# A hybrid attention and mixture-of-experts block on one core: narrow projection first, index scores earlier, subtractions from GpSimd to VectorE, and one transposition a projection later

## The chip, the cores and the metric

One core of a Trainium2 chip runs the whole kernel. The metric is the device time in microseconds of one execution. Engines: TensorE (PE, with its weight loads PEld), VectorE (DVE), ScalarE (ACT), GpSimd (POOL) and SyncE (SP), whose queue issues nearly all transfers.

## The reference, cut to what matters

One layer over 256 tokens of width 1024, all in float32:

```python
proj = x @ w_in                       # columns: A's q, c_kv, q_idx, k_idx, w_idx, B's q, k, v, two gates
# A: index scores pick 64 keys per token, then attention over the picked keys in the latent space
logits = relu(einsum('bthd,bsd->bths', q_idx, k_idx))
iscore = einsum('bth,bths->bts', w_idx * IDX_SCALE, logits)
_, sel = top_k(where(admissible, iscore, -inf), 64)
# ... softmax over the selected keys with a distance penalty, times c_kv, times w_uv -> y_A
# B: attention over all keys of earlier chunks, with a relative-position bias -> y_B
merged = sigmoid(gate_A) * (y_A @ w_branch_a) + sigmoid(gate_B) * (y_B @ w_branch_b)
x = layer_norm(ALPHA * x + merged @ w_out)
# top 4 of 32 experts per token, each a clamped SwiGLU with three 1024 x 1024 matrices
x = layer_norm(ALPHA * x + moe(x))
```

## The kernel before

All engines work through queues in the order in which the program is written out by hand; nothing is reordered at run time. SBUF is cut into 27 slots of 1 MB (`slot`, `free`). A list `pending` holds every large weight matrix in chunks of 1 MB, in order of use: 16 chunks of `w_in` (`in0` to `in15`, two per projection), two each of the branch matrices (`bb`, `ba`), four of `w_out` (`wo`), then the 12 chunks of each of 32 experts, some 403 of the 437.5 MB that are read. `load_next` (line 85) issues the next chunk on SP's queue. `pump(reserve)` issues chunks while more than `reserve` slots are left by the program's own count, and `used()` calls it after each chunk that has been multiplied, with the next number of `RESERVE`. A load whose slot is still being read waits in SP's queue, and what stands behind it too.

The projections and the branches are multiplied in a rounded format with correction: `split` writes a rounded copy `hi` (line 182, by ACT's copy at line 178) and the remainder `lo` (line 183), and each product is three matmuls, hi times hi, lo times hi, hi times lo. `ahead(n)` splits weight chunks up to number n; `AHEAD` says how far ahead of the chunk in use, and the letter in `LO_ENGINE` which engine subtracts (V for DVE, G for GpSimd). A chunk is two instructions of 128x1024 on ACT and two on the subtracting engine. `LO_MERGED` has the same letters for the merged rows before `w_out`.

The order on TensorE before the experts: `qi`, the index queries from `w_qi` (three of the eight steps over the width in plain float32, line 244, five in split form, line 247); `g0`, a narrow product of 200 columns for `k_idx`, `w_idx` and `c_kv` (line 253); `project_T(0)` (B's q); four transposes `ktr` (line 347) of the normalised `k_idx` and `c_kv`, from which DVE makes `kiT` and `ckT` (line 349); `project_T(1)` (B's k); the index scores (line 333), which ACT passes through relu and DVE sums per head (line 364) and searches for the 64 largest (lines 385 and 386); `kat` and `va` (lines 373 and 377); `project_T(2)` to `project_T(4)` with B's and A's scores among them; `project(5)` (B's values); `turn(sB, 1)`, which transposes B's probabilities (24 transposes, line 446); `project_T(6)`; `attend(vb, 1)` (line 462); `project_T(7)`; `turn(sA, 0)`; the two branches, between whose chunks `attend(va, 0)` stands; `w_out`; router; experts. `normalise` (line 423) divides the exponentials by their sums on DVE ahead of each `turn`.

The loads at the start: `xT` in five pieces on SP's queue and `w_qi` in five on ACT's, side by side; then `g0`, four chunks of `w_in`, and the small `ikgb` and `wuk` on SP's.

Of the kernel before, what the change touches and what calls it, by code (L numbers as in the profile page):

```python
# [15 lines left out]
NT = 2  # L16
D = 1024
KD = 8
# [11 lines left out]
SLOT_BASE = 1000.0  # L30
NSLOT = 27
QI_NATIVE = 3
LO_MERGED = "GVGV"
RESERVE = (4, 3, 3, 3, 4, 5, 3, 3, 3, 1, 3, 3, 3, 2, 3, 1, 2, 4, 3, 1, 5, 1, 1, 1, 0)
AHEAD = (3, 4, 3, 3, 3, 3, 3, 3, 3, 3, 3, 3, 3, 3, 3, 3, 3, 3, 3, 3, 3, 3, 2, 1, 0)
LO_ENGINE = "GVVGGGGGGGGGGVGVGVGVGVVV"
KEYS = (128, 256)
KOFF = (0, 128)

# [11 lines left out]
def body(nc, tc, slots, sm, psp, xT_d, x_d, w_g0, w_qi, w_in, ikgb_d, wuk_d,  # L51
# [7 lines left out]
    def slot(name):  # L59
        state["used"] += 1  # L60
        assert state["used"] <= NSLOT, name
        return slots.tile([128, 2048], F32, name=name, tag="slot")

    def free(n=1):
        state["used"] -= n
# [5 lines left out]
    def bank(name):  # L71
        return psp.tile([128, 512], F32, name=name, tag="ps")
# [7 lines left out]
    def load_next(eng=SP):  # L80
        key, src = pending.pop(0)
        t = slot("ld")
        state["ld"] += 1
        for part, from_ in src(t) if callable(src) else ((t, src),):
            eng.dma_start(part, from_)  # L85
        loaded[key] = t
# [44 lines left out]
    xT_s = slot("xT")  # L131
# [2 lines left out]
    wq = [t.rearrange("p (k c) -> p k c", k=4) for t in wq_s]  # L134
    g0_s = slot("g0")
    g0 = g0_s[:, :1600].rearrange("p (k c) -> p k c", k=KD)
    for k0, n in ((0, 1), (1, 1), (2, 2), (4, 2), (6, 2)):
        SP.dma_start(xT[:, k0:k0 + n, :], xT_d[:, k0:k0 + n, :])
        A.dma_start(wq[k0 // 4][:, k0 % 4:k0 % 4 + n, :], w_qi[:, k0:k0 + n, :])
    SP.dma_start(g0, w_g0)  # L140
    for _ in range(4):
        load_next()


    ident = sm.tile([128, 128], F32, name="ident")
# [3 lines left out]
    kvg = ikgb[:, 2:3]  # L149
    uku_s = slot("uku")  # L150
    SP.dma_start(uku_s[:, 0:1024], wuk_d)
    wr = sm.tile([128, KD, NE], F32, name="wr")
    rrow = sm.tile([1, NE], F32, name="rrow")
    lnc = sm.tile([128, 2, KD], F32, name="lnc")
    wuk = uku_s[:, 0:512]
# [18 lines left out]
    def vcopy(o, i):  # L174
        V.tensor_copy(o, i)

    def acopy(o, i):
        A.activation(o, i, AF.Copy)  # L178

    def split(t, hi, lo, rnd=acopy, sub=G):  # L180

        rnd(hi.bitcast(F32R), t)
        sub.tensor_tensor(lo.bitcast(F32R), t, hi, op=ALU.subtract)  # L183
# [6 lines left out]
    def ahead(n):  # L190

        for key in order[len(halves):n]:
            t = take(key)
            hi, lo = slot("hi"), slot("lo")
            sub = {"V": V, "G": G}[LO_ENGINE[len(halves)]]
            for h in range(2):
                cs = slice(h * 1024, (h + 1) * 1024)
                split(t[:, cs], hi[:, cs], lo[:, cs], sub=sub)
            halves.append((hi, lo))
            done(1)  # L200
# [30 lines left out]
    wqh = [slot("wqh0"), slot("wqh1")]  # L231
    wql = [slot("wql0"), slot("wql1")]
    wqHL = [[t.bitcast(F32R).rearrange("p (k c) -> p k c", k=4) for t in ts] for ts in (wqh, wql)]
    qp = [bank("qi") for _ in range(4)]
    for k in range(KD):
        sl = slice(k * 256, (k + 1) * 256)
        split(xT_s[:, sl], xh_s[:, sl], xl_s[:, sl], vcopy, V)
        if k >= QI_NATIVE:
            sl = slice(k % 4 * 512, (k % 4 + 1) * 512)
            split(wq_s[k // 4][:, sl], wqh[k // 4][:, sl], wql[k // 4][:, sl])  # L240
        for j in range(4):
            js = slice(j * 128, (j + 1) * 128)
            if k < QI_NATIVE:
                PE.matmul(qp[j][:, 0:256], wq[k // 4][:, k % 4, js], xT[:, k, :], start=(k == 0), stop=False)
                continue
            for a, b in THREE:
                PE.matmul(qp[j][:, 0:256], wqHL[b][k // 4][:, k % 4, js], xHL[a][:, k, :],
                          start=False, stop=(k == KD - 1 and b == 1))
    free(6)
    g0ps = [bank("g0ps") for _ in range(NT)]  # L250
    for k in range(KD):
        for tb in range(NT):
            PE.matmul(g0ps[tb][:, 0:200], xT[:, k, tb * 128:(tb + 1) * 128], g0[:, k, :],
                      start=(k == 0), stop=(k == KD - 1))
    free(2)
    V.scalar_tensor_tensor(negd, negd, -1.0, negd, op0=ALU.mult, op1=ALU.min)

    def project(g, sink):
# [14 lines left out]
    def project_T(g, sink):  # L273

        ps = [bank("fm") for _ in range(2)]
        for c in range(2):
            i = IN + 2 * g + c
            ahead(i + 1 + AHEAD[i])
            for j in range(4):
                for k in range(4):  # L280
                    for a, b in THREE:
                        PE.matmul(ps[j // 2][:, j % 2 * 256:j % 2 * 256 + 256], part(i, b, k, 4)[:, j * 128:(j + 1) * 128],  # L282
                                  xHL[a][:, 4 * c + k, :], start=(c + k + a + b == 0 and j % 2 == 0),
                                  stop=(c == 1 and k == 3 and b == 1), skip_group_check=True)
                if c == 1 and j % 2:
                    sink(slice(j - 1, j + 1), ps[j // 2].rearrange("p (j t) -> p j t", j=2))
            used()

    def copy_to(dst):
        return lambda js, p: acopy(dst[:, js, :], p)  # L290

    ahead(AHEAD[0])
    for j in range(4):
        vcopy(qiT[:, j, :], qp[j][:, 0:256])


    kT_s = slot("kidxT_ckvT")
# [39 lines left out]
                     ps.rearrange("p (i n) -> p i n", i=per))  # L337


    qb_s = slot("qb")  # L340
    qbT = qb_s[:, 0:1024].rearrange("p (j t) -> p j t", j=4)
    kbT = qb_s[:, 1024:2048].rearrange("p (j t) -> p j t", j=4)
    project_T(0, copy_to(qbT))
    p = bank("ktr")
    for tb in range(NT):
        for i in range(2):
# [8 lines left out]
    def relu_sink(tb, heads, ps):  # L355
        A.activation(rl[tb][:, heads[0]:heads[-1] + 1:2, :], ps, AF.Relu)

    project_T(1, copy_to(kbT))
    for tb in range(NT):
        head_scores(qiT, lambda j: kiT, tb, relu_sink)  # L360
        sl = slice(KOFF[tb], KOFF[tb] + KEYS[tb])
# [4 lines left out]
    free(2)  # L366

    va = uku_s[:, 1024:2048].rearrange("p (b c) -> p b c", b=2)
    for j2 in range(2):
        p = bank("kat")  # L370
        for jj in range(2):
            j = 2 * j2 + jj
            PE.matmul(p[:, jj * 256:(jj + 1) * 256], wuk[:, j * 128:(j + 1) * 128], ckT, start=True, stop=True)
        acopy(kaT[:, 2 * j2:2 * j2 + 2, :], p.rearrange("p (j t) -> p j t", j=2))
    for sb in range(NT):
        p = bank("va")
        PE.matmul(p, ckT[:, sb * 128:(sb + 1) * 128], wuv, start=True, stop=True)
# [17 lines left out]
        SP.dma_start(t, d)  # L395
    SP.dma_start(b1_s, relb_d[:, 1024:3072])
    SP.dma_start(b0_s[:, 0:1024], relb_d[:, 0:1024])
    project_T(2, copy_to(qaT))


# [13 lines left out]
    def exps(s, w):  # L414
        for tb in range(NT):
            for h in range(H):
                A.activation(s[tb][:, h, :], s[tb][:, h, :], AF.Exp, bias=mx[:, w, tb, h:h + 1],
                             accum_out=sums[:, w, tb, h:h + 1])
# [12 lines left out]
    def gate_sink(w, n):  # L431
        return lambda js, p: A.activation(sg[w][:, 4 * n + js.start:4 * n + js.stop, :], p, AF.Sigmoid)
# [57 lines left out]
    project(5, lambda tb, p: acopy(vb[:, tb, :], p))  # L490
    normalise(sB, 1)
    exps(sA, 0)
    turn(sB, 1)
    free(2)
    project_T(6, gate_sink(1, 0))
    attend(vb, 1)
    normalise(sA, 0)
    project_T(7, gate_sink(1, 1))
    free(2)
    turn(sA, 0)  # L500
    free(2)

# [596 lines left out]
```

## Time and profile before

| | |
|---|---|
| median of 3 runs | 1137.94 us (1136.99 to 1138.29) |
| the profiled execution | 1137.62 us, of which the span of its instructions is 1136.0 us |
| TensorE busy | 1061.2 us (93%) |
| DVE, ACT, POOL busy | 293.4, 228.7, 96.6 us |
| read from memory | 435.48 MB, 384 GB/s over the span |
| mean granted clock of TensorE | 0.985 |

Times in the rows are microseconds from the start of the span unless they are marked ns. A busy TensorE is not one at its peak, since matmuls are pipelined and their ends modelled. The granted clock is 1.00 at 2.4 GHz and 0.50 at 1.2 GHz.

### The profile page before, as it was taken

What the parts mean: (1) busy time and instruction counts of PE and PEld (TensorE: products, weight loads), DVE (VectorE), ACT (ScalarE), POOL (GpSimd) and SP (SyncE); (2) the same over time, 40 slices, a digit from 0 to 9 for tenths busy, and PEclk for the clock granted to TensorE, in tenths of its full rate; (3) what the DMA queues carried; (4) which work ended last, traced back from release to release, by engine and by line L of the source; (5) the groups of instructions that cost most, each with busy time, mean ns of one, the idle gap of its engine ahead of it and who ended that gap; (6) DMA issues with size and microseconds to landing.
All of it is one profiled execution on the core that took longest, in us unless ns stands there. A gap on an engine that the chain in (4) does not pass through costs nothing. (4 is left out here: it accounts for less than half of the span.)

```text
span 1136.0 us, 13723 instructions
## 1 busy us (share of the span) xinstructions
PE 1061.2 (93%) x5599; PEld 535.3 (47%) x5599; DVE 293.4 (26%) x711; ACT 228.7 (20%) x425; POOL 96.6 (9%) x54
## 2 busy tenths in 40 slices
PE   8998999999999999999999988996999999989985
PEld 8997998543434343434343434342434343333432
DVE  5398556322111111111111111111021102011123
ACT  3557542211111111201111101111111111011112
POOL 4675232000000000000000000000000000000001
PEclk9999999999999999999999999998999999998998
DMA  9925477999999999999999999999999999999994
GB/s 361 419 108 221 149 267 293 404 399 420 421 421 421 422 420 421 420 422 421 420 422 421 421 421 421 421 421 419 421 421 421 422 421 421 421 407 421 421 419 173
DMA packets 63932, 437.52 MB, mean 385 GB/s; under 512 B 7252, under 2 KB 7892, under 8 KB 11892
## 3 DMA queue, kind: packets, MB, share of 16 engines
q1 hardware_dynamic: 62998, 434.20, 92.9%
q10 hardware_dynamic: 864, 2.36, 0.6%
q8 instruction: 47, 0.77, 0.3%
q14 instruction: 23, 0.19, 0.0%
HBM read 435.48 MB, written 1.05 MB: 384 GB/s over the span
## 5 line engine op out<-in xcount | busy, mean ns | idle before, releaser
L777 PE MATMUL gu<-ld,wa 128*64 128x512 f32 x1024 | 460.1, 602 | 28.9 <-DMA ld<-in_dram 28.9
L775 PE MATMUL gu<-ld,wa 128*64 128x512 f32 x1024 | 458.9, 601 | 7.0 <-PEq L851 3.8
L809 PE MATMUL y<-ld,wc 128*64 128x512 f32 x992 | 239.2, 596 | 16.3 <-DMA ld<-in_dram 16.3
L775 PEld LDWEIGHTS gu<-ld,wa 128*64 128x64 f32 x1024 | 135.8, 138 | 226.5 <-issue 219.7
L796 DVE TENSOR_TENSOR wc<-tr,wb 128x256 f32<-128x256 f32 x64 | 27.0, 421 | 706.6 <-PE tr L792 706.6
L777 PEld LDWEIGHTS gu<-ld,wa 128*64 128x64 f32 x1024 | 135.2, 138 | 112.7 <-DMA ld<-in_dram 60.3
L809 PEld LDWEIGHTS y<-ld,wc 128*64 128x64 f32 x992 | 77.0, 136 | 164.6 <-issue 122.2
L178 ACT ACTIVATE wb<-gu 128x512 f32<-128x512 f32 x64 | 38.2, 597 | 445.1 <-PE gu L775 232.9
L178 ACT ACTIVATE wc<-y 64x512 f32<-64x512 f32 (+1 forms) x66 | 38.2, 578 | 224.2 <-PE y L809 216.7
L183 POOL TENSOR_TENSOR lo<-ld,hi 128x1024 fp32r<-128x1024 f32 x30 | 76.5, 2575 | 62.6 <-ACT hi L178 50.3
L984 POOL PARTITION_BROADCAST ln<-ln x1 | 2.3, 2298 | 929.0 <-DMA ld<-in_dram 929.0
L651 PEld LDWEIGHTS ga<-wa,x 128*128 128x128 f32 x512 | 61.6, 196 | 12.3 <-issue 12.2
L651 PE MATMUL ga<-wa,x 128*128 128x128 f32 x512 | 64.8, 285 | 0.0
L282 PE MATMUL fm<-xh,hi 128*128 128x256 f32 x224 | 64.3, 287 | 0.0
L282 PE MATMUL fm<-xl,hi 128*128 128x256 f32 x224 | 63.4, 283 | 0.0
L282 PE MATMUL fm<-xh,lo 128*128 128x256 f32 x224 | 63.4, 283 | 0.0
L821 PE MATMUL sum<-wc,wb 128*128 128x512 f32 x120 | 54.0, 592 | 0.0
L178 ACT ACTIVATE hi<-ld 128x1024 fp32r<-128x1024 f32 x48 | 47.5, 1048 | 26.8 <-PE fm L282 12.3
L282 PEld LDWEIGHTS fm<-xh,hi 128*128 128x128 f32 x224 | 42.9, 192 | 0.7 <-issue 0.4
L282 PEld LDWEIGHTS fm<-xl,hi 128*128 128x128 f32 x224 | 43.0, 192 | 0.2 <-issue 0.2
L282 PEld LDWEIGHTS fm<-xh,lo 128*128 128x128 f32 x224 | 43.0, 192 | 0.0
L798 ACT ACTIVATE wa<-wc 128x256 f32<-128x256 f32 x64 | 26.6, 416 | 79.4 <-DVE wc L797 78.8
(235 smaller groups left out, 828.6 us busy)
## 6 DMA issues: line engine op xcount, KB each, us to landing
ld<-in_dram SPq DMA_DIRECT2D x404, 1024.0 KB, 19.8
ld<-in_dram SPq DMA_DIRECT2D x8, 512.0 KB, 13.7
wq<-in_dram ACTq DMA_DIRECT2D x3, 512.0 KB, 7.8
biasB<-in_dram SPq DMA_DIRECT2D x1, 1024.0 KB, 12.1
x<-in_dram SPq DMA_DIRECT2D x1, 1024.0 KB, 6.8
g<-in_dram SPq DMA_DIRECT2D x1, 800.0 KB
xT<-in_dram SPq DMA_DIRECT2D x3, 256.0 KB, 7.5
out_dram<-acc SPq DMA_DIRECT2D x3, 256.0 KB, 2.0
```

The source lines that it names most:

```text
L178: A.activation(o, i, AF.Copy)
L183: sub.tensor_tensor(lo.bitcast(F32R), t, hi, op=ALU.subtract)
L282: PE.matmul(ps[j // 2][:, j % 2 * 256:j % 2 * 256 + 256], part(i, b, k, 4)[:, j * 128:(j + 1) * 128], xHL[a][:, 4 * c + k, :], start=(c + ...
L651: PE.matmul(ps[j // per][:, (j % per) * n:(j % per + 1) * n], x1_cols(tb, j), Pt, start=(tb == 0 and j % per == 0), stop=(tb == 1), skip_g ...
L775: PE.matmul(ps[n][0:64, :], xe(j), wg(j, cs), start=(j == 0), stop=(j == KD - 1), skip_group_check=True)
L777: PE.matmul(ps[n][64:128, :], xe(j), wu(j, cs), start=(j == 0), stop=(j == KD - 1), skip_group_check=True)
L796: V.tensor_tensor(gg, pv[:, :, 0, :], bg(js), op=ALU.add)
L798: A.activation(sg_, gg, AF.Sigmoid, scale=1.702)
L809: PE.matmul(p[64 * n:64 * n + 64, :], hT[:, j, :], wd(j, slice(n * 512, (n + 1) * 512)), start=(j == 0), stop=(j == KD - 1), skip_group_ch ...
L821: PE.matmul(sums[tb][n], lhsT, rhs, start=start, stop=stop, skip_group_check=True)
L984: G.partition_broadcast(ln2_s, ln2_s[0:1, :])
```

## The change

It loads `xT` and `g0` first (`g0` on ACT's queue, `w_qi` behind `xT` on SP's, the four chunks after `wuk`) and multiplies `g0` ahead of `qi`. `ktr`, the split of `in0` and `kat` come before `project_T(0)`; the index scores, the search and `va` come between `project_T(0)` and `project_T(1)`. DVE subtracts 21 of the 24 chunks in place of 9, all of `qi`'s five steps and all four merged groups. `turn(sB, 1)` comes after `project_T(6)` in place of `project(5)`, and `attend(vb, 1)` after `project_T(7)`. Two of the reserves change.

```diff
-LO_MERGED = "GVGV"
-RESERVE = (4, 3, 3, 3, 4, 5, 3, 3, 3, 1, 3, 3, 3, 2, 3, 1, 2, 4, 3, 1, 5, 1, 1, 1, 0)
+LO_MERGED = "VVVV"
+RESERVE = (4, 1, 3, 3, 4, 5, 3, 3, 3, 1, 3, 3, 3, 3, 3, 1, 2, 4, 3, 1, 5, 1, 1, 1, 0)
-LO_ENGINE = "GVVGGGGGGGGGGVGVGVGVGVVV"
+LO_ENGINE = "VVVVVGGGVVVVVVVVVVVVVVVV"
...
-    for k0, n in ((0, 1), (1, 1), (2, 2), (4, 2), (6, 2)):
+    for k0, n in ((0, 1), (1, 1), (2, 2), (4, 4)):
         SP.dma_start(xT[:, k0:k0 + n, :], xT_d[:, k0:k0 + n, :])
-        A.dma_start(wq[k0 // 4][:, k0 % 4:k0 % 4 + n, :], w_qi[:, k0:k0 + n, :])
-    SP.dma_start(g0, w_g0)
-    for _ in range(4):
-        load_next()
+    for k0, n in ((0, 2), (2, 6)):
+        A.dma_start(g0[:, k0:k0 + n, :], w_g0[:, k0:k0 + n, :])
+    for k0, n in ((0, 2), (2, 2), (4, 4)):
+        SP.dma_start(wq[k0 // 4][:, k0 % 4:k0 % 4 + n, :], w_qi[:, k0:k0 + n, :])
...
     SP.dma_start(uku_s[:, 0:1024], wuk_d)
+    for _ in range(4):
+        load_next()
...
+    g0ps = [bank("g0ps") for _ in range(NT)]
+    for k in range(KD):
+        for tb in range(NT):
+            PE.matmul(g0ps[tb][:, 0:200], xT[:, k, tb * 128:(tb + 1) * 128], g0[:, k, :],
+                      start=(k == 0), stop=(k == KD - 1))
+        sl = slice(k * 256, (k + 1) * 256)
+        split(xT_s[:, sl], xh_s[:, sl], xl_s[:, sl], vcopy, V)
+    free(1)
     qp = [bank("qi") for _ in range(4)]
     for k in range(KD):
-        sl = slice(k * 256, (k + 1) * 256)
-        split(xT_s[:, sl], xh_s[:, sl], xl_s[:, sl], vcopy, V)
+        sl = slice(k % 4 * 512, (k % 4 + 1) * 512)
         if k >= QI_NATIVE:
-            sl = slice(k % 4 * 512, (k % 4 + 1) * 512)
-            split(wq_s[k // 4][:, sl], wqh[k // 4][:, sl], wql[k // 4][:, sl])
+            split(wq_s[k // 4][:, sl], wqh[k // 4][:, sl], wql[k // 4][:, sl], sub=V)
...
-    free(6)
-    g0ps = [bank("g0ps") for _ in range(NT)]
-    for k in range(KD):
-        for tb in range(NT):
-            PE.matmul(g0ps[tb][:, 0:200], xT[:, k, tb * 128:(tb + 1) * 128], g0[:, k, :],
-                      start=(k == 0), stop=(k == KD - 1))
-    free(2)
+    free(7)
...
-    ahead(AHEAD[0])
-    for j in range(4):
-        vcopy(qiT[:, j, :], qp[j][:, 0:256])
...
-    project_T(0, copy_to(qbT))
     p = bank("ktr")
...
-    project_T(1, copy_to(kbT))
+    ahead(1)
+    for j in range(4):
+        (acopy if j % 2 else vcopy)(qiT[:, j, :], qp[j][:, 0:256])
+    for j2 in range(2):
+        p = bank("kat")
+        for jj in range(2):
+            j = 2 * j2 + jj
+            PE.matmul(p[:, jj * 256:(jj + 1) * 256], wuk[:, j * 128:(j + 1) * 128], ckT, start=True, stop=True)
+        acopy(kaT[:, 2 * j2:2 * j2 + 2, :], p.rearrange("p (j t) -> p j t", j=2))
+    project_T(0, copy_to(qbT))
     for tb in range(NT):
         head_scores(qiT, lambda j: kiT, tb, relu_sink)
...
+    project_T(1, copy_to(kbT))
     project_T(2, copy_to(qaT))
...
     project(5, lambda tb, p: acopy(vb[:, tb, :], p))
     normalise(sB, 1)
     exps(sA, 0)
+    project_T(6, gate_sink(1, 0))
     turn(sB, 1)
     free(2)
-    project_T(6, gate_sink(1, 0))
-    attend(vb, 1)
     normalise(sA, 0)
     project_T(7, gate_sink(1, 1))
     free(2)
+    attend(vb, 1)
     turn(sA, 0)
     free(2)
```

## Rows read from the trace of the kernel before

**Rows 1.** Busy time by stretch: engines, granted clock, DMA share, rate.

```profile
0.00:60.00 60.00, 56.29 (x405) 52.65 (x406) 27.64 (x60) 28.95 (x42) 33.07 (x24) 0.97 0.96 384
60.00:195.00 135.00, 129.29 (x1032) 121.70 (x1031) 96.31 (x155) 63.22 (x123) 58.34 (x28) 0.97 0.54 204
195.00:1118.00 923.00, 868.47 (x4134) 358.25 (x4132) 160.17 (x484) 133.32 (x255) 1.82 (x1) 0.99 1.01 418
```

**Rows 2.** Waits of TensorE from 420 us on: total, times, longest.

```profile
PE gu L777 <- DMA ld<-in_dram: 28.9, 28, 1.4
```

**Rows 3.** Timeline of TensorE around `turn(sB)` and `project_T(6)`: start, length.

```profile
109.00 0.39 PE L267 MATMUL tm<-lo,xh 128*128 128x512 f32 x1
111.56 0.79 PE L446 MATMUL ptr<-ident,biasB 128*128 128x128 f32 x4 [2.17 <-DVE biasB L423]
...
119.39 0.36 PE L282 MATMUL fm<-xh,hi 128*128 128x256 f32 x1
...
131.07 2.84 PE L462 MATMUL pv<-pt,sa_vb 128*64 128x128 f32 x48
```

**Rows 4.** The same timeline at `turn(sA)` and the first branch.

```profile
145.46 0.60 PE L446 MATMUL ptr<-ident,sa_vb 128*128 128x128 f32 x4
...
148.00 0.48 PE L528 MATMUL br<-y,hi 128*128 128x256 f32 x2
```

**Rows 5.** Busy time by stretch, at the start and at `turn(sB)`.

```profile
16.00:20.00 4.00, 4.00 (x23) 4.00 (x22) 0.00 (x0) 3.07 (x5) 3.20 (x3) 0.57 1.01 419
109.40:119.40 10.00, 4.30 (x25) 3.97 (x25) 8.15 (x5) 8.28 (x35) 4.09 (x2) 0.66 0.00 0
```

**Rows 6.** Timeline of DVE at the two calls of `normalise`.

```profile
108.15 7.48 DVE L423 TENSOR_TENSOR biasB<-biasB,sums 128x1024 f32<-128x1024 f32 x2
...
135.58 1.22 DVE L423 TENSOR_TENSOR sa_vb<-sa_vb,sums 128x1024 f32<-128x1024 f32 x1
136.73 2.28 DVE L423 TENSOR_TENSOR sa<-sa,sums 128x2048 f32<-128x2048 f32 x1
```

**Rows 7.** Timeline of ACT at the last exponential of `sA`.

```profile
116.44 0.49 ACT L417 ACTIVATE sa<-sa,mx 128x256 f32<-128x256 f32 x1
```

**Rows 8.** The subtractions of line 183: ns min/median/max, first and last start.

```profile
L183 POOL TENSOR_TENSOR lo<-ld,hi x30: 2352/2407/5135, 20.1 to 157.9; 128x1024 fp32r<-128x1024 f32 x30
L183 DVE TENSOR_TENSOR lo<-ld,hi x18: 1211/1219/3379, 21.0 to 180.2; 128x1024 fp32r<-128x1024 f32 x18
L183 DVE TENSOR_TENSOR y<-pv,y x4: 691/692/692, 133.4 to 157.6; 128x512 fp32r<-128x512 f32 x4
```

**Rows 9.** Timeline of DVE at the first residual.

```profile
186.64 0.69 DVE L669 SCALAR_TENSOR_TENSOR x<-x,wo 128x512 f32<-128x512 f32 x1 [5.20 <-PE wo L665]
```

**Rows 10.** Busy time by stretch in the first 20 us, rate last.

```profile
0.00:10.00 10.00, 8.06 (x50) 7.24 (x51) 3.10 (x12) 1.91 (x2) 1.69 (x9) 1.00 0.78 252
10.00:20.00 10.00, 8.23 (x46) 7.17 (x45) 5.51 (x11) 4.22 (x7) 6.23 (x5) 0.83 1.02 423
```

**Rows 11.** Timelines of DVE and ACT where they wait for `xT` and `w_qi`.

```profile
9.01 0.29 DVE L175 CAST xh<-xT 128x256 fp32r<-128x256 f32 x1 [1.94 <-DMA xT<-in_dram]
...
16.93 1.15 ACT L178 ACTIVATE wqh<-wq 128x512 fp32r<-128x512 f32 x2 [2.64 <-DMA wq<-in_dram]
```

**Rows 12.** Timelines of TensorE and DVE from `qi` to `ckT`.

```profile
8.59 2.54 PE L244 MATMUL qi<-xT,wq 128*128 128x256 f32 x11
...
22.43 5.58 PE L253 MATMUL g0ps<-g,xT 128*128 128x200 f32 x32
27.70 0.42 PE L282 MATMUL fm<-xh,hi 128*128 128x256 f32 x1
...
39.36 0.60 PE L347 MATMUL ktr<-ident,kidxT_ckvT 128*128 128x128 f32 x4
39.71 0.36 PE L282 MATMUL fm<-xh,hi 128*128 128x256 f32 x1
...
40.46 0.48 DVE L349 TENSOR_SCALAR kidxT_ckvT<-ktr,ikgb 128x256 f32<-128x256 f32 x1
```

More of the change, by code (lines that the diff above doesn't have):

```diff
@@ L337, in head_scores @@
                      ps.rearrange("p (i n) -> p i n", i=per))
-    qb_s = slot("qb")
-    qbT = qb_s[:, 0:1024].rearrange("p (j t) -> p j t", j=4)
-    kbT = qb_s[:, 1024:2048].rearrange("p (j t) -> p j t", j=4)
-    project_T(0, copy_to(qbT))
     p = bank("ktr")
@@ L356, in relu_sink @@
         A.activation(rl[tb][:, heads[0]:heads[-1] + 1:2, :], ps, AF.Relu)
-    project_T(1, copy_to(kbT))
+    ahead(1)
[7 more added lines that the diff above has]
+        acopy(kaT[:, 2 * j2:2 * j2 + 2, :], p.rearrange("p (j t) -> p j t", j=2))
+    qb_s = slot("qb")
+    qbT = qb_s[:, 0:1024].rearrange("p (j t) -> p j t", j=4)
+    kbT = qb_s[:, 1024:2048].rearrange("p (j t) -> p j t", j=4)
+    project_T(0, copy_to(qbT))
     for tb in range(NT):
@@ L368, in body @@
     va = uku_s[:, 1024:2048].rearrange("p (b c) -> p b c", b=2)
[L369 to L374, printed above, removed]
     for sb in range(NT):
```

## The prediction, made before the changed kernel ran

> **What bounds the kernel now.** I read the stretches first: from 195 to 1118 us the DMA engines are busy without a pause, 418 GB/s at share 1.01 [rows 1]. What TensorE waits for after 420 us is those transfers: on the gate and up line alone 28 waits, 28.9 us, none over 1.4 [rows 2]. So the expert weights set the end: it is the moment from which the stream never pauses again, plus bytes that the change leaves alone. Before that moment the stream does pause: from 60 to 195 us its share is 0.54 [rows 1], some 62 us without transfers, because the 27 slots are full and come free only as TensorE finishes chunks. So a microsecond taken out of TensorE's queue before about 200 us should bring the whole stream, and the end, forward by one; work moved between other engines counts only if TensorE waits for it.
>
> Then I read where TensorE loses time before 200 us. One place stands out. The last matmul of `project(5)` ends at 109.39, `turn(sB)` gets its first four transposes off at 111.56, and `project_T(6)` starts at 119.39 [rows 3]: 10.00 us. The same 24 transposes of `turn(sA)` take from 145.46 to 148.00, 2.54 us [rows 4]. The loss is 7.46 us, part of it at half the matrix rate, since the granted clock of the stretch is 0.66 and TensorE's busy time 4.30 of 10; the DMA share there is 0.00 [rows 5], so the stream stands still with TensorE. What is late is `normalise(sB)` on DVE: 7.48 us from 108.15 to 115.63, against 1.22 + 2.28 = 3.50 us for the same shapes of `sA` [rows 6]; GpSimd, busy for 4.09 us of the stretch [rows 5], was subtracting beside it.
>
> **The turning one projection later.** `project_T(6)` takes 119.39 to 131.07, 11.68 us [rows 3]. Put ahead of `turn(sB)`, it moves the transposes from 109.39 to 121.07, while `normalise(sB)` ended at 115.63: covered by 5.4 us even at the slow length. I count the whole 7.46 us. What can be late next: ACT ends the exponentials of `sA` at about 117 [rows 7], then rounds `in15` and `bb0` (four instructions, 3.9 us), loads the sigmoid table (1.3) and evacuates `project_T(6)` (2 x 0.6), done at 123.4; `project_T(7)`, which may take those two banks again, starts at 121.07 + 2.54 = 123.6. That holds by 0.2 us, so between nothing and 1 us can come back here; I take nothing, because the first bank is free 0.5 us sooner. `attend(vb, 1)` now ends right before `turn(sA)`; its two casts and two subtractions are four DVE instructions of 0.69 us [rows 8], the first branch chunk reads only the first half, and 2.54 us of transposes lie between. Nothing, or 0.5 us. The pages that hold B's probabilities come free later, which shifts two loads by one projection each, in a stretch where the stream is idle about half the time.
>
> **The subtractions.** 12 of the 24 chunks go from GpSimd to DVE, 24 instructions of 1.22 us = 29.3; seven of half the size (five of `qi`'s, two of the merged rows) at 0.69, 4.8. Together 34 us. GpSimd keeps three chunks, 6 x 2.41 us [rows 8]. DVE is busy 27.6 + 96.3 = 124 us of the first 195 [rows 1]; with 34 added and the 4.0 us excess of `normalise(sB)` taken off, some 154 of 188. It is in-order, so the average doesn't settle it; three places do.
> First, the stretch up to the turning: `in11`, `in12` and `in14` add 3 x 2.44 = 7.3 us in front of `normalise(sB)`. If not one of them fell into idle time, it would end at 115.63 + 7.3 - 4.0 = 118.9, before 121.07. If this cover went, each microsecond would be one of TensorE's.
> Second, the top-k. It starts one projection earlier (11.6 us) and has three more chunks (`in8` to `in10`, 7.3 us) behind it before B's scores need DVE: free 4 us sooner than now.
> Third, the output projection: two merged groups more wait in DVE's queue for ACT's rounding (0.7 each) and subtract (0.7): 2.8 us, so the last chunk's subtraction, which ends at 181.4 now, ends at about 184.2. It is needed some 1.4 us ahead of 186.64, where the residual follows the last matmuls [rows 9]: covered by 1 us. Between nothing and 1 us; I take nothing.
> What speaks against the move is that GpSimd's three remaining chunks run beside the top-k. The longest DVE subtraction took 3.38 us against 1.21 [rows 8]. The Trainium skill (SBUF — State Buffer, Who interferes with whom) says that a DVE instruction with two SBUF inputs and a GpSimd instruction that reads SBUF exclude each other, the later one blocked for the whole of the other; the row agrees. By that rule six GpSimd instructions could hold DVE for 6 x 2.41 = 14.5 us here, an estimate; but the rows that I sum from already hold more GpSimd work beside the same top-k, so the sum is the same either way.
>
> **The start.** Bytes: 2.52 MB had moved by 10 us and the rate is then 423 GB/s [rows 10], so x us moves 0.42 (x - 4) MB. The third piece of `xT` ends 0.52 MB on SP's queue, and its companion of `wq` 1.05 MB on ACT's; it landed at 9.01 [rows 11], 1.3 us after 1.57 MB had moved. In the new order `g0` (0.82 MB, ACT's queue) shares with `xT` (1.05 MB, SP's): at equal shares `g0` is through at 1.64 MB, 7.9 us, and lands at 9.1; `xT` at 9.7. (The last of `wq`, 2.1 MB on ACT's queue, landed at 16.93 [rows 11], when 4.9 MB had moved: a share of 43%, by which `g0` lands at 9.8.) TensorE can do two of eight steps early and starts the other six at 9.1. `g0`'s 16 matmuls took 22.43 to 27.70 [rows 12], 0.33 each, so 12 take 4.0 us: 13.1. `qi`'s 12 native matmuls: 11 records in 2.54 us, so 24 records 5.5 us: 18.6. The 60 rounded ones at the pace of `project_T(6)`, 11.68/96 = 0.122 [rows 3], 7.3 us: 25.9. `wq` is through by 3.97 MB, landed at 14.7, and the rounding and subtraction of its last four steps by 18, so they hide. Then `ktr`, which now has nothing between it and `kat`: transposes at 39.36, `ckT` ready at 40.94, 1.58 us, where before only 0.35 us of TensorE's queue was spent [rows 12]. `in0`'s subtraction now comes behind `ckT` on DVE, 1.2 us to its first half, and `kat`'s four matmuls cover it. Against the first chunk's start now (27.70, plus the 0.35): 28.05 - (25.9 + 1.58) = 0.6 us gained at the full clock.
> But TensorE then idles from about 7 to 9.1 us. Two rows tell what follows a pause of that size: after the idle 13 to 15 us the clock from 16 to 20 us was 0.57 [rows 5], a loss of 0.43 x 4 = 1.7 us, and after 109.39 it fell too. I take the half clock: 0.6 - 1.7 = -1.1 us. Ends: +0.6 with the clock held, -2.6 if `g0` lands 1.5 us later.
> Moving scores and `kat` costs TensorE nothing in itself: the same instructions, with banks evacuated by an ACT that has room there (29 busy of the first 60 us [rows 1]).
>
> **Sum.** 7.46 - 1.1 = 6.4 us, rounded up. From the profiled execution's 1137.62 us (span 1136.0 and 1.6 around it): 1131.2. That execution stands 0.3 us under the median of the runs, 1137.94, so I leave the figure there.
>
> **The rivals.**
> 1. The clock holds at the start (or falls where TensorE waits anyway): 7.46 + 0.6 gives 1129.6.
> 2. The turning still waits: ACT is late with the sigmoids, or DVE's longer queue uses up the 2 us that [rows 6] leave it. A wait of 1 to 4 us gives 1132.2 to 1135.2. For it: DVE has little room in that stretch. Against it: 11.68 us of cover.
> 3. The time is not carried to the end: slots come free as before, by another engine than TensorE, and the stream starts no earlier: 1137.6. Against it: it moved nothing at all in the stall [rows 5].
> 4. Slower, by one mechanism: `g0` on ACT's queue doesn't get half of the rate but is served behind SP's. Behind `xT` and `wq` it would land at 4 + 3.97/0.42 + 1.25 = 14.7 us, 5.6 late, and the gain shrinks to 0.8 us (1136.8); from a landing at 15.5 the kernel is slower; behind `wuk` and `in0` as well (5.54 MB) it lands at 18.4, 9.3 late: 1140.5. Against it: ACT's 43% above [rows 11].
>
> **How the numbers follow.** My forecast, the turning's 7.46 us less 1.1 at the start, 45 in 100; rival 1, 22; rival 2, 20; rival 3 and rival 4 up to its point, 6; rival 4 beyond it, or DVE so late that it outweighs 6.4 us, 7. The range takes the forecast, rival 1 with 0.7 us to spare, and rival 2 up to a wait of 3 us: 1128.8 to 1134.3, 83 in 100 or a little less. A difference of 0.2% (2.3 us) is about what a measurement of this kernel can tell from no change. Faster by more than that: 87; within it: 6; slower: 7.
>
> **What would show it.** Right: `project_T(6)` follows `project(5)` without a gap, `turn(sB)` takes about 2.5 us, `turn(sA)` ends near 141.5 in place of 148.0, and the stream is at share 1.0 from some 6 us sooner; a granted clock under 1 once near 10 us; DVE busy for some 154 us before 190. Wrong: a wait of `ptr` for `sB`, of the first chunk for `lo`, or of `g0ps` for `g0` past 10 us; an equal time with an earlier `turn(sA)` would mean that the stream isn't led by TensorE.

## The result, and the profile after

The changed kernel takes 1127.96 us (median of 4 runs, 1127.57 to 1129.88), the kernel before beside it 1138.08 (4 runs, 1136.99 to 1138.29): a ratio of 0.9916, 95% interval 0.9899 to 0.9934. It is faster, as forecast, but by 10.1 us in place of 6.4; the time lies 0.8 us under the low end of the range. The profiled execution happens to be the longest of the four, 1129.88 us, with a span of 1128.3; a second profile of the same kernel (`after_again`, 1128.07 us) stands beside it below, because the two differ at one place. Helper lines sit two lines further down than before: the subtractions are L185, the transposes L448, `project_T` L284.

The stretches of the changed kernel, columns as in [rows 1]:

```profile
0.00:60.00 60.00, 56.50 (x407) 53.37 (x408) 40.42 (x100) 29.80 (x44) 12.67 (x13) 1.00 0.95 384
60.00:187.00 127.00, 127.00 (x1031) 120.08 (x1029) 100.60 (x143) 62.65 (x123) 7.97 (x8) 1.00 0.58 216
187.00:1110.00 923.00, 870.02 (x4136) 358.17 (x4133) 160.55 (x485) 133.51 (x255) 2.30 (x1) 0.99 1.01 418
```

From 60 to 187 us TensorE has no idle time at all (127.00 of 127; 129.29 of 135 before). The stream of transfers is at share 1.01 over the same 923 us set 8 us sooner than in [rows 1], and has the rate that it had, 418 GB/s. The waits of TensorE, of the first 215 us (the two longest behind the start-up) and, last, from 420 us on:

```profile
PE kat L359 <- issue: 1.1, 1, 1.1
PE g0ps L239 <- DMA xT<-in_dram: 0.6, 1, 0.6
...
PE gu L779 <- DMA ld<-in_dram: 28.7, 26, 1.6
```

No wait of `ptr` is left, and the waits for expert weights are those of [rows 2], 28.7 us against 28.9: the second part of the kernel didn't change, it begins sooner. That can be checked to a few tenths. TensorE's first expert matmul starts at 209.86 in the trace of before, and that execution's whole time is 927.8 us more; in the changed kernel it starts at 202.01, with 927.9 us more to the whole time; in its second profile at 199.97, with 928.1 more:

```profile
199.97 0.64 PE L777 MATMUL gu<-ld,wa 128*64 128x512 f32 x1
```

So the 9.9 us between 209.86 and 199.97 are the gain from trace to trace, and it arises at two places only: before B's turning (the scores of `sA` start at 95.40 before, at 93.18 in the second profile, 2.2 sooner) and at it (from those scores to `turn(sA)`: 50.06 us before, 42.34 in both profiles after, 7.7 less). From `turn(sA)` to the first expert matmul it takes 64.4 or 64.5 us in all fourteen profiles. The 2.2 us are a difference to one trace, though: `turn_only` below, whose start is that of before, has those scores at 93.40.

The turning, timeline of TensorE and, last, of DVE, for [rows 3] and [rows 6]:

```profile
108.83 0.39 PE L269 MATMUL tm<-lo,xh 128*128 128x512 f32 x1
109.05 0.28 PE L284 MATMUL fm<-xh,hi 128*128 128x256 f32 x1
```

```profile
110.19 3.43 DVE L425 TENSOR_TENSOR biasB<-biasB,sums 128x1024 f32<-128x1024 f32 x2
```

The first matmul of `project_T(6)` follows the last of `project(5)` on its heels, where 10.00 us stood. `turn(sB)` starts 11.5 us later, at 120.57, and its 24 transposes take 2.54 us. `normalise(sB)` takes 3.43 us where it took 7.48 and is done at 113.6: 7 us ahead of its reader.

The start is where the two profiles of the changed kernel differ. TensorE in the first, and then in the second (each of `g0`'s 16 matmuls is two records):

```profile
5.04 1.65 PE L239 MATMUL g0ps<-g,xT 128*128 128x200 f32 x4
7.25 6.89 PE L239 MATMUL g0ps<-g,xT 128*128 128x200 f32 x28 [0.56 <-DMA xT<-in_dram]
13.98 1.24 PE L252 MATMUL qi<-xT,wq 128*128 128x256 f32 x5
```

```profile
5.04 1.31 PE L239 MATMUL g0ps<-g,xT 128*128 128x200 f32 x4
6.95 5.15 PE L239 MATMUL g0ps<-g,xT 128*128 128x200 f32 x28 [0.60 <-DMA xT<-in_dram]
11.94 3.40 PE L252 MATMUL qi<-xT,wq 128*128 128x256 f32 x15
```

The wait is the same, 0.6 us, and it is for `xT`, not for `g0`. The 28 records behind it take 6.89 us in one and 5.15 in the other; one microsecond of each, the first profile's and then the second's, shows why:

```profile
10.00:11.00 1.00, 1.00 (x4) 1.00 (x4) 0.93 (x4) 0.00 (x0) 0.00 (x0) 1.00 1.10 459
```

```profile
10.00:11.00 1.00, 1.00 (x8) 1.00 (x7) 0.95 (x3) 0.00 (x0) 0.00 (x0) 1.00 1.12 467
```

Four records a microsecond against eight, TensorE busy all the time: half the rate, until 10.9 us. It isn't the pause that brings it. In the first profile the four records ahead of the pause are as far apart (0.33 us) as those behind it, so TensorE had not come to the full rate yet. Two more profiles of the new start, `after_third` and then `start_only`, have the same four records at the half rate and at the full one, a pause of 0.29 us and one of 1.06, and the full rate behind both:

```profile
5.04 1.65 PE L239 MATMUL g0ps<-g,xT 128*128 128x200 f32 x4
6.98 5.09 PE L239 MATMUL g0ps<-g,xT 128*128 128x200 f32 x28 [0.29 <-DMA xT<-in_dram]
```

```profile
4.94 0.94 PE L239 MATMUL g0ps<-g,xT 128*128 128x200 f32 x4
6.95 5.00 PE L239 MATMUL g0ps<-g,xT 128*128 128x200 f32 x28 [1.06 <-DMA xT<-in_dram]
```

All that follows is 2.04 us later in the first profile, to the end of the kernel. Of eight profiles of kernels that load `g0` in the new way one shows this; of the thirteen executions of the changed kernel itself one, this one, is over 1128.6 us.

The subtractions: DVE is busy 147.4 us of the first 195 in the second profile (154 reckoned, 124 before), GpSimd 20.8 (91.4 before, [rows 1]). The chunks' subtractions in the first profile (busy, mean ns | idle before):

```profile
L185 DVE TENSOR_TENSOR lo<-ld,hi 128x1024 fp32r<-128x1024 f32 x42 | 50.7, 1266 | 7.4 <-ACT hi L180 7.4
```

42 of them at 1.27 us, and none delays TensorE. The last two stand in front of the residual of [rows 9] (timeline of DVE):

```profile
173.39 4.33 DVE L185 TENSOR_TENSOR lo<-ld,hi 128x1024 fp32r<-128x1024 f32 x2 [0.26 <-ACT hi L180]
178.79 0.69 DVE L671 SCALAR_TENSOR_TENSOR x<-x,wo 128x512 f32<-128x512 f32 x1 [1.07 <-PE wo L667]
```

The second of them ends at 177.72, and the matmul that reads it starts at 178.37: 0.65 us to spare, 1 reckoned.

### The profile page after: what moved, and what is told of

Its sections match the earlier page's. It is cut to its first block, busy times and chain, and to the rows that moved or that the text cites. A ratio compares the mean times of both kernels' runs of the same rounds, so it can differ in the third digit from the quotient of the medians.

```text
span 1128.3 us, 13701 instructions
## 1 busy us (share of the span) xinstructions
PE 1060.8 (94%) x5599; PEld 534.3 (47%) x5599; DVE 310.8 (28%) x740; ACT 229.2 (20%) x427; POOL 25.8 (2%) x23
## 5 line engine op out<-in xcount | busy, mean ns | idle before, releaser
L779 PE MATMUL gu<-ld,wa 128*64 128x512 f32 x1024 | 459.3, 601 | 30.8 <-DMA ld<-in_dram 28.7
L284 PE MATMUL fm<-xh,hi 128*128 128x256 f32 x224 | 64.1, 286 | 0.0
L284 PE MATMUL fm<-xl,hi 128*128 128x256 f32 x224 | 63.4, 283 | 0.0
L284 PE MATMUL fm<-xh,lo 128*128 128x256 f32 x224 | 63.4, 283 | 0.0
L185 DVE TENSOR_TENSOR lo<-ld,hi 128x1024 fp32r<-128x1024 f32 x42 | 50.7, 1266 | 7.4 <-ACT hi L180 7.4
L284 PEld LDWEIGHTS fm<-xh,hi 128*128 128x128 f32 x224 | 43.0, 192 | 0.6 <-ACT hi L180 0.3
L284 PEld LDWEIGHTS fm<-xl,hi 128*128 128x128 f32 x224 | 43.0, 192 | 0.3 <-issue 0.2
L284 PEld LDWEIGHTS fm<-xh,lo 128*128 128x128 f32 x224 | 43.0, 192 | 0.0
L794 PEld LDWEIGHTS tr<-ident,wb 128*128 128x128 f32 x256 | 33.3, 208 | 13.7 <-issue 12.6
## 6 DMA issues: line engine op xcount, KB each, us to landing
biasB<-in_dram SPq DMA_DIRECT2D x1, 1024.0 KB, 11.5
```

The source lines that it names most:

```text
L779: PE.matmul(ps[n][64:128, :], xe(j), wu(j, cs), start=(j == 0), stop=(j == KD - 1), skip_group_check=True)
L794: PE.transpose(p[:, i * 128:(i + 1) * 128], gu[:, (j // 2) * 256 + j % 2:(j // 2) * 256 + 256:2], ident)
```

## The experiments

None of these kernels leaves out a part of the computation; `before_warm` only adds matmuls whose result nobody reads. Times are medians; the ratio is to the kernel before, run on the same chip (1138.46, 1138.58 and 1138.22 us in the three groups of runs).

**The changed kernel again.**

> The changed kernel once more, unchanged, for more executions and a second trace. Its profiled execution reached the first expert 7.85 us sooner than before and ended 7.74 sooner, but the median of its runs is 10.1 us lower than that of before. Theory 1 (only TensorE's queue before the experts counts): the trace shows the first expert again 7.8 +- 0.3 us sooner, at about 202.0, and the medians differ by 7.5 to 8.5 with more runs, the rest being scatter of single runs. Theory 2 (the start differs from run to run in what the clock does, and the profiled run was a bad one): the first expert starts 1 to 2 us before 202.0 and the medians differ by 9 to 10.5. Theory 3 (something in the experts' stage gets shorter too): the first expert at 202.0, but the end 2 us sooner than 1128.3 of span, and the medians differ by about 10.

1128.32 us (1127.71 to 1128.5), 0.9911 (0.9897 to 0.9924). The time repeats. Its profile is the one quoted above; the scores of `sA` start at 93.18.

**The turning alone, in the kernel before**, with the one reserve that belongs to it.

```
     exps(sA, 0)
+    project_T(6, gate_sink(1, 0))
     turn(sB, 1)
     free(2)
-    project_T(6, gate_sink(1, 0))
-    attend(vb, 1)
     normalise(sA, 0)
...
     free(2)
+    attend(vb, 1)
     turn(sA, 0)
```

> The kernel before with one part of the change alone: the turning of B after the projection behind it, attend one projection later, the one reserve that belongs to it. Theory 1: 7.46 us at the first expert (202.4), 1130.5 +- 1 of time, so nearly the whole difference; the two normalisations keep their lengths. Theory 2 and 3 with the gain elsewhere: still 7.5 here, and the missing 2 us then come with another part. If the cover failed: a wait of the transposes for normalise and less than 6 us.

1129.95 us (1128.88 to 1131.1), 0.9929 (0.9915 to 0.9943): 8.5 us by the medians. This edit carries most of the whole. From the scores of `sA` to `turn(sA)` it takes 42.34 us, as in the whole change. `normalise(sB)` is as slow as it was, because GpSimd still subtracts beside it (timeline of DVE):

```profile
106.15 7.57 DVE L423 TENSOR_TENSOR biasB<-biasB,sums 128x1024 f32<-128x1024 f32 x2
```

It ends at 113.7, and `turn(sB)` starts at 118.74 without a wait: 5.0 us of cover, 5.4 reckoned.

The start of this kernel is that of before, instruction for instruction, and yet its trace is 2.0 us ahead of that of before when `g0` begins (22.43 in [rows 12]) and when the scores of `sA` do (93.40 against 95.40). The last piece of `w_qi` is there at 15.51 (16.93 in [rows 11]), and the clock holds where [rows 5] has 0.57:

```profile
20.42 5.58 PE L253 MATMUL g0ps<-g,xT 128*128 128x200 f32 x32
```

```profile
16.00:20.00 4.00, 3.48 (x29) 3.28 (x29) 0.50 (x2) 2.97 (x5) 3.78 (x3) 1.00 1.02 422
```

So the old start differs by 2 us from one execution to another, and the trace that the forecast was reckoned from has a late one.

**The subtractions alone, in the kernel before.**

```
-LO_MERGED = "GVGV"
+LO_MERGED = "VVVV"
-LO_ENGINE = "GVVGGGGGGGGGGVGVGVGVGVVV"
+LO_ENGINE = "VVVVVGGGVVVVVVVVVVVVVVVV"
...
-            split(wq_s[k // 4][:, sl], wqh[k // 4][:, sl], wql[k // 4][:, sl])
+            split(wq_s[k // 4][:, sl], wqh[k // 4][:, sl], wql[k // 4][:, sl], sub=V)
```

> The kernel before with the subtractions of the change alone (21 chunks, the five steps of qi and the merged rows on DVE), all orders as before. normalise(sB) should fall from 7.48 to about 3.5 us with GpSimd silent, and end at about 113.6 in place of 115.6. Theory 1: TensorE's stall at the turning shrinks by 2 to 3.5 us, the start by up to 1 us (the wait for wql on GpSimd, 1.0 us, goes), so 1134 to 1136. If DVE's queue is the dearer place (it is longer by 29 us): equal or slower, 1138 to 1140.

1137.35 us (1136.13 to 1138.21), 0.9991 (0.9982 to 1.0). TensorE's timeline at the turning before (the wait for the later transposes, behind the one in [rows 3]), then here, and then DVE's here:

```profile
115.89 3.75 PE L446 MATMUL ptr<-ident,biasB 128*128 128x128 f32 x20 [3.54 <-DVE biasB L423]
```

```profile
112.32 1.09 PE L446 MATMUL ptr<-ident,biasB 128*128 128x128 f32 x4 [4.33 <-DVE biasB L423]
114.51 4.50 PE L446 MATMUL ptr<-ident,biasB 128*128 128x128 f32 x20 [1.11 <-DVE biasB L423]
```

```profile
106.02 4.62 DVE L183 TENSOR_TENSOR lo<-ld,hi 128x1024 fp32r<-128x1024 f32 x4
110.56 0.24 DVE L421 RECIPROCAL sums<-sums 128x16 f32<-128x16 f32 x1
110.83 3.43 DVE L423 TENSOR_TENSOR biasB<-biasB,sums 128x1024 f32<-128x1024 f32 x2
```

`normalise(sB)` is 4.1 us shorter but starts 2.7 later (110.83 against 108.15 of [rows 6]), behind two chunks that GpSimd did before. It ends 1.4 us sooner, but `project(5)` does too. The two waits are 4.33 and 1.11 us in place of 2.17 and 3.54, 5.4 in all against 5.7, and from the scores of `sA` to `turn(sA)` it takes 50.90 us against 50.06: quick DVE work doesn't help while TensorE asks for it right behind `project(5)`.

**The whole change without the new start** (loads as before, `g0` behind `qi`).

```
-    for k0, n in ((0, 1), (1, 1), (2, 2), (4, 4)):
+    for k0, n in ((0, 1), (1, 1), (2, 2), (4, 2), (6, 2)):
         SP.dma_start(xT[:, k0:k0 + n, :], xT_d[:, k0:k0 + n, :])
-    for k0, n in ((0, 2), (2, 6)):
-        A.dma_start(g0[:, k0:k0 + n, :], w_g0[:, k0:k0 + n, :])
...
+        A.dma_start(wq[k0 // 4][:, k0 % 4:k0 % 4 + n, :], w_qi[:, k0:k0 + n, :])
+    SP.dma_start(g0, w_g0)
...
```

> The changed kernel with the start of before: w_qi on ACT's queue beside xT, g0 and four chunks behind, and g0 multiplied after qi; all else as changed. Theory 1: the start before lost 1.7 us to the half clock and 1.7 to waits, and the changed one starts its first projection only 0.25 us sooner, so 0.2 to 1 us slower than the changed kernel, 1128.5 to 1131 beside 1128 to 1130. Theory 2 (the start is worth 2 us more than the profiled run showed): 2 to 3 us slower than the changed kernel.

1136.98 us (1136.16 to 1138.11), 0.999 (0.9981 to 0.9999): 8.7 us above the changed kernel, far outside what either theory said. The timeline of TensorE:

```profile
20.27 5.58 PE L253 MATMUL g0ps<-g,xT 128*128 128x200 f32 x32
29.66 1.22 PE L339 MATMUL ktr<-ident,kidxT_ckvT 128*128 128x128 f32 x4 [3.81 <-DVE kidxT_ckvT L314]
31.95 3.75 PE L357 MATMUL kat<-kidxT_ckvT,uku 128*128 128x256 f32 x8 [1.07 <-issue]
```

With `ktr` next in the queue behind `g0`, TensorE stands 3.81 us for the norms of `g0`'s result and 1.07 for `ckT` (the view names no releaser, but `ckT` is written by 31.85 and `kat` starts at 31.95), and it works at half rate between the two and behind (`kat`'s eight matmuls 3.75 us against 1.97 in the changed kernel). The scores of `sA` start at 101.56, 8.4 us behind `after_again`. The kernel before hid the norms under `project_T(0)`; the changed one hides them under `qi`, which now comes after `g0`. Start and new place of `ktr` and `kat` are one edit, not two.

**The whole change with B's turning in its old place** (the diff of `turn_only` reversed).

> The changed kernel with the turning of B back in its old place (and attend and the one reserve). In the run with only the subtractions moved the stall there was 10.8 us for 2.5 us of transposes, because the longer queue of DVE ends normalise(sB) 6 us behind project(5) although normalise itself is down to 3.4. Theory (the turning is the main gain, and the subtractions need it): the stall returns whole, 6 to 8.3 us slower than the changed kernel, 1134.5 to 1136.8. Rival (the quiet GpSimd had shortened the stall by half on its own): 3 to 4 us slower, 1131.5 to 1132.5.

1134.62 us (1133.63 to 1135.91), 0.997 (0.9961 to 0.9979): 6.3 us above `after_again`. TensorE's waits of the first 215 us:

```profile
PE ptr L448 <- DVE biasB L425: 4.0, 2, 2.5
```

From the scores of `sA` to `turn(sA)` 49.67 us against 42.34, so 7.3 come back, 4.0 of them as this wait and the rest at half rate beside and behind it (granted clock 0.66 from 110 to 120).

**The new start alone, in the kernel before.** The edit is the start's part of the change (printed above): loads, `g0` ahead of `qi`; `ktr`, `kat` and the scores stay.

> The kernel before with the new start alone: xT and g0 loaded and multiplied first, w_qi and four chunks behind; ktr, kat, scores, turning and subtracting engines as before. Theory: no pause of 2 us in the middle of qi, so the loss to waits (1.7) goes always and the one to the half clock (1.7, which fell in the profiled run of before and not in three later ones) goes too: 1 to 2.5 us faster than before in the median, and a narrower spread. Rival (the start is worth what the two first traces differ by): 0.2 us, not to be told from before.

1136.8 us (1135.68 to 1138.49), 0.9985 (0.9976 to 0.9994): 1.7 us, between 0.7 and 2.7. TensorE has the scores of `sA` at 92.78: 2.6 us ahead of the trace of before and 0.6 ahead of `turn_only`, the old start at its better. It is also 0.4 ahead of `after_again`. Of that, 0.15 is an earlier `qi` (11.79 against 11.94); the other 0.25 is what the new places of `ktr`, `kat` and the index scores cost TensorE.

**The kernel before with its TensorE kept busy at the start**, by 24 small matmuls ahead of each of two steps of `qi`.

```
+        if k in (4, 5):
+            warm(24)
         for j in range(4):
```

> The kernel before with 24 more small matmuls on zeros ahead of the fifth and of the sixth step of qi, where TensorE waits for w_qi, and nothing else; the result is not touched by them. It tells the clock from the waits. If the spread of before is the half clock that falls in some runs after that pause: the clock holds at 1.00 in the first 30 us, the slowest runs (1139 to 1140) go, and the median falls by 0.5 to 1.7 us. If the clock has no part in it: same as before or up to 1 us slower.

1138.33 us (1136.96 to 1139.22), 1.0001 (0.9992 to 1.001). The stretch of [rows 5] has its clock, and `g0` comes no sooner all the same (22.43 in [rows 12]):

```profile
16.00:20.00 4.00, 4.00 (x48) 3.96 (x47) 0.00 (x0) 2.94 (x4) 3.06 (x3) 1.00 1.00 412
```

```profile
22.34 5.58 PE L255 MATMUL g0ps<-g,xT 128*128 128x200 f32 x32
```

This run doesn't settle what the clock was worth: the second filler runs from 16.63 to 17.95, while the remainder that the next step reads was ready at 16.83, so it took 1.1 us itself. A better reading is `dve_only`, where the last piece of `w_qi` landed at the same time (16.87 us; 16.93 in [rows 11]) and the clock held by itself: `g0` at 21.02, 1.4 us sooner. There the subtractions of `w_qi` were quicker too, so 1.4 is a bound from above. In `turn_only` GpSimd subtracts as before, the last piece came 1.4 us sooner and `g0` 2.0: that leaves 0.6 for the clock, from one execution of each.

**`kat` later:** in the changed kernel, `ktr` after the first chunk's rounding and `kat` behind `project_T(0)` and the index scores, run twice.

```
+    ahead(1)
     p = bank("ktr")
...
-    ahead(1)
     for j in range(4):
         (acopy if j % 2 else vcopy)(qiT[:, j, :], qp[j][:, 0:256])
-    for j2 in range(2):
...
     va = uku_s[:, 1024:2048].rearrange("p (b c) -> p b c", b=2)
+    for j2 in range(2):
```

> The changed kernel with one thing more: in0 is split ahead of ktr (DVE idles there for 4.5 us), and kat comes behind project_T(0) and the index scores, so that TensorE doesn't wait the 1.07 us between ktr and kat that both traces of the changed kernel show. If only TensorE's queue counts: 1.0 us faster than the changed kernel, about 1127.2, the first project_T starts right behind ktr. Rival: the first chunk's remainder is late instead and the wait only moves: same.

> The kernel with in0 split ahead of ktr and kat behind the index scores once more, beside the changed kernel on one chip: 1.0 to 1.3 us faster than that, as the first experts (198.7 against 200.0) say. If that was the chip or the single run: same.

1127.0 (1126.47 to 1128.06) and 1127.01 us (1126.71 to 1127.58), 0.991 (0.9895 to 0.9925) and 0.9904 (0.989 to 0.9919). TensorE goes from `ktr` into the projection without a pause, and its first expert matmul comes at 198.72 and 198.47:

```profile
24.36 0.60 PE L342 MATMUL ktr<-ident,kidxT_ckvT 128*128 128x128 f32 x4
24.72 0.36 PE L284 MATMUL fm<-xh,hi 128*128 128x256 f32 x1
```

That is the wait of `kat` (1.07 us), and this version is 1.0 us ahead of the changed kernel that ran beside the second of them (`after_third`, 1128.04): below what the ratios' intervals can tell apart, but seen in the first expert matmul as well.

**The whole change with the subtractions on their old engines** (the diff of `dve_only` reversed).

> The changed kernel with the subtractions where they were (15 chunks, qi's five steps and two merged groups on GpSimd). GpSimd then slows normalise(sB) to 7.5 us again, but project_T(6) lies over it. Theory (the subtractions buy nothing of their own once the turning is later): same as the changed kernel within 0.7 us, DVE's busy time down and GpSimd's up by some 70 us. Rival (they are needed): one of the first chunks is late, GpSimd at 4.8 us a chunk before project_T(0), or qi waits for GpSimd's five remainders: 1.5 to 4 us slower than the changed kernel, with waits for lo or wql in the trace.

1129.27 us (1128.35 to 1130.58), 0.992 (0.9907 to 0.9933), from five executions; a sixth, of 6055 us, is left out. DVE 134.0 us of the first 195, GpSimd 91.3, `normalise(sB)` back at 7.56 us, and TensorE's timeline is that of `after_again` to a hundredth: scores of `sA` at 93.19, `turn(sA)` at 135.52, first expert at 199.98. So the subtractions' place gives TensorE nothing before the experts. The profiled execution still ends 930.6 us behind its first expert matmul, not 928, and the median is 1.2 us above the changed kernel's beside it, between the two theories. Whether that is the subtractions' doing stays open; what is different after 200 us I haven't found.

**`g0` behind `xT` and `w_qi` on SP's queue**, the mechanism of the rival that ended slower.

```
-    for k0, n in ((0, 2), (2, 6)):
-        A.dma_start(g0[:, k0:k0 + n, :], w_g0[:, k0:k0 + n, :])
     for k0, n in ((0, 2), (2, 2), (4, 4)):
         SP.dma_start(wq[k0 // 4][:, k0 % 4:k0 % 4 + n, :], w_qi[:, k0:k0 + n, :])
+    for k0, n in ((0, 2), (2, 6)):
+        SP.dma_start(g0[:, k0:k0 + n, :], w_g0[:, k0:k0 + n, :])
```

> The changed kernel with g0 loaded last of the three, behind xT and w_qi on SP's queue, still multiplied first. This is the mechanism by which the prediction saw the change turn slower. Theory (the start is set by when the first loads land): g0 lands near 14 us in place of 7, the first expert comes 6 to 8 us later than with the changed kernel and the end by the same, 1134 to 1136.5. Rival (the waiting is made up because the rounding of w_qi and the subtractions run ahead meanwhile, or by idle places further on): 2 to 4 us later at the first expert, 1130.5 to 1132.5.

1137.48 us (1136.58 to 1140.51), 0.9995 (0.9986 to 1.0003): the whole gain is gone.

```profile
13.78 7.11 PE L239 MATMUL g0ps<-g,xT 128*128 128x200 f32 x32 [8.53 <-DMA g<-in_dram]
```

The matmuls wait 8.53 us for `g0` and then run at half rate until 16.7 (7.11 us against 5.58 for the same 32 in [rows 12]); the first expert comes at 208.75, 8.8 behind `after_again`.

**The changed kernel a third time**, beside the last three.

> The changed kernel, to be compared with the three others of this call: about 1128.2, the first expert at 200.0, or at 202.0 if TensorE runs at the half rate until about 11 us as in the first of its traces.

1128.04 us (1127.74 to 1128.54), 0.9913 (0.9899 to 0.9927); scores of `sA` at 93.15, first expert at 199.94.

## Why the prediction was right in its direction and short in its size

**That TensorE's queue before the experts sets the end** held, and in numbers: of fourteen profiles, eleven end 927.7 to 928.2 us after their first expert matmul, whatever was done before it (`turn_only` 928.7, `start_only` 930.1, `dve_undone` 930.6 are the others). Rival 3, a gain not carried to the end, is out.

**The turning, 7.46 us**, was the right mechanism and nearly the right size: 7.7 in the traces (50.06 less 42.34), 8.5 in `turn_only` by the medians, 6.3 by the medians and 7.3 in the traces when it is undone. From the scores of `sA` to `turn(sA)` it takes 42.34 us in all nine profiles with the new order and 49.67 to 51.57 in the five with the old one. Part of that spread is the half rate behind the stall, which lasts now longer, now shorter: in the trace of before the granted clock is back at 1.00 by 119 us, in that of `before_warm` at 122, and there the stretch takes 51.57 us. The price of a stall in one execution is a sample. The cover held too, so rival 2 (the turning still waits) didn't come; the reckoned worst end of `normalise(sB)`, 118.9, was 113.6. That it is 4.1 us shorter without GpSimd beside it, 3.43 against 7.48 in the trace of before, 7.57 in `turn_only` and 7.56 in `dve_undone`, bears out the row that the prediction read. The Trainium skill (SBUF — State Buffer, Who interferes with whom) says that a DVE instruction with two SBUF inputs, as `normalise` is, and a GpSimd instruction that reads SBUF exclude each other; `turn_only` and `after` agree with that, at 7.57 and 3.43 us.

**The step that failed is "The start", with its sum of 0.6 - 1.7 = -1.1 us.** In its place the runs show a gain: 1.7 us (0.7 to 2.7) for the start alone in `start_only`; from trace to trace 2.2 us in the second profile and 0.2 in the first, against the trace of before. Two terms of it were off.
First, the landing of `g0`. I let it share equally with `xT` and had TensorE wait for it to 9.1 us. No profile of the changed kernel shows a wait for `g0`; TensorE waits 0.6 us for the second piece of `xT`, goes on at 6.95 and begins `qi` at 11.94, where 13.1 was reckoned. The first steps of `qi`, in plain float32, take 4.99 us where 5.5 was reckoned. So `ktr` starts at 24.30 where 25.9 was reckoned at the full clock: 1.6 us, of which 1.2 are `g0`'s. In `start_only`, the one trace that shows it, the larger piece of `g0` lands 5.4 us after its issue at 1.3. Why it came sooner than equal shares of the bytes would bring it, no run here tells.
Second, the clock. I took a fall to the half clock as certain, because the one row I had, [rows 5], showed it behind a pause of TensorE. No profile of the new start shows such a fall, nor the sign that I gave for it, a granted clock under 1 near 10 us. All eight begin at the half rate: the small matmuls on zeros ahead of `g0` are 0.107 us apart, and 0.055 where `start_only` has come to the full rate. Seven come to it between 5 and about 7 us and have it behind a pause of 0.3 to 1.1 us. The first profile of the changed kernel came to it at 10.9 only; why, these runs don't tell. That it lost 2.04 us, 0.3 of it by later data, near the 1.7 that I had put down for the pause, is luck. What a pause of the two microseconds that I reckoned with would have done, these runs don't show. Nor did the half clock cost 1.7 us where I had read it: in the trace of before it is at most 1.4 by `dve_only`, and 0.6 by `turn_only`. Nor was [rows 5] the rule for the old start: in four more profiles of it (`turn_only`, `dve_only`, `start_undone`, `before_warm`) the clock from 16 to 20 us is 1.00.
1.6 and 1.7 are the 3.3 us that the start was better than forecast, and with the turning's 0.3 they are nearly all of the difference between 6.4 and 10.1. But they are reckoned against a trace of before with a late start. Against `turn_only` the second profile has the scores of `sA` only 0.2 us sooner. So, as far as these traces tell, what the new start buys is less a quicker best case than that the old one's late executions go away; that is read from few executions and not tested. Rival 1, the clock that holds (1129.6 us), was nearest, and short by the same 1.6.

**Rival 4**, `g0` late, didn't come. Made to come true in `g0_behind`, it has about the price that I gave it, and takes the whole gain: the new start rests on `g0` not standing behind `xT` and `w_qi`.

**The subtractions at nothing** was right for TensorE up to the experts: `dve_undone` has the same timeline to a hundredth. By themselves they give at most 2 us (`dve_only`, 0.9982 to 1.0). The three places that I named as near had 7.0 us to spare, no wait, and 0.65. At the third I had overlooked GpSimd: the last subtraction takes 3.19 us beside a broadcast on GpSimd (174.08 to 176.78), in `dve_undone`, where it is over before the broadcast, 1.21.

**The scores and `kat`** were counted as nothing, with a latency of 1.58 us behind `ktr` in the start's sum; TensorE idles 1.07 there, and `kat_later` gets about that back. What I had not seen is how much this move needs the new start: on the old one it costs 7 to 8 us (`start_undone` against `turn_only`, 1136.98 and 1129.95 us, scores of `sA` at 101.56 and 93.40).

**Do the parts add up?** Alone they give 8.5, 1.7 and 1.1 us by the medians, 11.3 together against 10.1 measured. `kat`'s 1.07 us of idle time, which none of the three holds, would make up the difference, but each of the three is uncertain by 1 to 1.6 us, so the sum can't show it. No run takes the moved index scores or the other changed reserve by itself.

## What to carry to other kernels

When TensorE leads a stream, look for the stretch where both stand still, and put a piece of independent TensorE work between the producer and the wait: 11 us of cover made the producer's slowness cost nothing, while making the producer itself twice as quick gave nothing at the stall. Price a stall and a clock loss from more than one execution, since the tail at half rate is not the same in each, and ask whether the one trace that a forecast starts from is a typical one. And undo every part from the finished kernel as well as adding it to the old one: the new place of `ktr` and `kat` cost 0.25 us on the new start and 7 to 8 on the old.

## What was not expected of the hardware

- In the first profile the granted clock reads 1.00 from 5 to 11 us, the higher of its two levels (2.4 GHz), while busy matmuls run at half rate, four records to the microsecond in place of eight. The Trainium skill (TensorE: Matmul & The Clock Gate, Seeing it yourself) warns that the profile's clock events can't always be trusted on this chip; here counting the instructions of a microsecond showed what the column did not.
- The same stall at the turning, in the same kernel but for matmuls 90 us earlier, had a tail at half rate that lasted 3 us longer (`before` and `before_warm`, granted clock 0.50 to 119 and to 122 us).
